# A scan level of 4 tokens back moved from the projections into the scans, queries read in place by the scans' products, and v blocks in the order 0, 2, 1, 3

## The chip, the cores and the metric

The kernel runs on one core of a Trainium2 chip. The metric is the device time of the whole kernel in microseconds (us). The engines are named as in the profile: PE is TensorE's matmul side and PEld its weight loads, DVE is VectorE, ACT is ScalarE, POOL is GpSimd, SP is SyncE, and a q behind a name (SPq, ACTq) is the queue from which that engine issues transfers. Each engine works through its own list of instructions strictly in order, so an instruction that waits holds up what stands behind it on its engine.

## The reference, cut to what matters

One layer on 128 context tokens and 1024 latent tokens, 1024 channels. A combined projection gives, for each of 8 heads of 128 channels, the queries q, two forget gates f (one for each direction), the values v and a gate z. Each direction runs a gated linear recurrence along the tokens:

```
S_t = diag(f_t) S_{t-1} + k_t v_t^T        k_t = 1 - f_t
o_t = S_t^T q_t
```

The reference works in chunks of 32 tokens, in which the pair of a token t and an earlier token s has the weight "q_t times k_s times the product of all f between them":

```
att = einsum('bhtc,bhsc,bhtsc->bhts', qi, ki, decay)
o   = einsum('bhts,bhsv->bhtv', att, vi) + einsum('bhtc,bhcv->bhtv', qi * exp(b), S)
```

A Fourier branch, output gates, two branch projections, one output projection and a norm follow. All of it is in float32.

## The kernel before

**Tiling.** The 1152 tokens are nine chunks of 128. Channels stand on the partitions, tokens on the free axis. Every dense product is split in three: a weight and an input are each a rounded high part and a low rest, and `mm3` (lines 205 to 211) issues high by high, low by high and high by low, in moving pieces of 288 tokens (256 for v).

**Stages.** First the statistics and the normalised input `h1`, `h2`; then the values, `project_v` (from line 398): v block `pr` holds the weights of two heads. The loop over `pr` in 0, 1, 2, 3 calls it; blocks 2 and 3 cover here only the chunks 5 to 8 (`LATE_V`), and the rest is done later among the scans. The split weights of a block (`w_hi` on ACT, line 184, `w_lo` on POOL, line 186) go to the pool `vb` for even and `va` for odd blocks, each with one buffer, so a block whose pool is still read by products has to wait with its split. Beside the v blocks, POOL, DVE and ACT build sums and differences of the input (`r`, line 427; `ts`, line 432; `t0` to `t3`, lines 434 and 435) that the next stage needs. In that stage 27 times `pair` computes two projections by seven products of 24 matmuls (`PRODUCTS`); the weights of a pair arrive as `raw`, are combined on DVE (line 636) and split (lines 618, 619).

**Steps among the projections.** Between the products of a pair the generator `four` is moved on by one step (the line with `next(four, None)`): first the Fourier branch, then `pieces`, which prepares the scans. A piece is one head and either 640 or 512 tokens, so there are 16. It loads f and q back from memory (lines 571 and 574), forms k = 1 - f (`L585`) and q times f (`L586`, `L587`), and then works by levels: the tokens that lie m back, for m = 1, 2, 4, are handled by pairs of blocks of m tokens. A level copies the halves of `kk` and `qq` that it needs side by side (`halves`, L470 on ACT), multiplies keys and queries by the gate product of the block (`grow`, L464 on DVE), doubles the gate blocks (L466), has 20 or 16 small products of 32 by 32 on PE (`within`, L484; each is two instructions in the trace, so x40 or x32), and merges their result by a mask (`merge`, L475 for the diagonal and L477). After the last grow it keeps a thinned gate product `fa` (L599, one in `GRAN` = 8 tokens) and issues the loads of the next piece's f, and after its last products that of the next q.

**The scans.** `scan_blocks` takes a head on from there over the levels 8 and 16 (`LATE`), with copies `km` and `qm` of 1152 tokens on ACT, `grow` over 1152 tokens, and 36 small products (x72), and then the levels 32 and 64, whose products read `kk` and `qq` in place. The state recurrence (`scan_rest`), the last chunks of v and the branch projections (`F`, a group of 12 matmuls of 288 tokens) are mixed with it by the strings of `PATTERN`: each letter moves one generator on by one step (E: blocks, L: the head before, Y: the rest of the head two before, V: late v, F: dense). PE keeps this written order in the scans. On the other engines the order of instructions comes from the scheduler of the framework, by priority and readiness.

Of the kernel before, what the change touches and what calls it, by code (L numbers as in the profile page):

```python
# [48 lines left out]
PRODUCTS = (1, 5, 6, 2, 7, 4, 3)  # L49
EARLY = (1, 2, 4)  # L50
GATES = 6
LATE = (8, 16)
GRAN = 8
PIECES = ((0, 640), (640, T))
PATTERN = (['VEVVEVVEVVEVV', 'VEVLVVLEVVLVVLEVVLVVLELFLF'] + 6 * ['EYLFYLEYLFLEFFFLEFLFLF'] +
           ['YLFYLFYLFLFFFLFLFLF', 'YFYFYFFF'])
# [13 lines left out]
def diffusion_step(ctx: ExitStack, tc: tile.TileContext, xT, x_tok, w_pr, w_v, w_ada, w_ada_gt,  # L70
# [326 lines left out]

    def project_v(pr, chunks):
        raw = vb.tile([P, KT, 2 * P], F32, tag="wr", name="w_raw")
        nc.sync.dma_start(raw, w_v[pr])  # L400
        hi, lo = split_w(raw, KT, 2 * P, (vb, va)[pr % 2])
        for c in chunks:
            ps = dense_ps()[:, :2 * P]
            mm3(ps, [(*h_at(k, c * P, (c + 1) * P), hi[:, k, :], lo[:, k, :]) for k in range(KT)])
            vo = va.tile([P, SW], F32, tag="vo", name="vo", bufs=2)[:, :2 * P].rearrange("p (h v) -> p h v", h=2)
            nc.vector.tensor_copy(vo, ps)
            nc.sync.dma_start(v_dr[2 * pr:2 * pr + 2, :, c, :].rearrange("h p v -> p h v"), vo)
# [8 lines left out]
    with pool("tg", 1, side="right") as tg:  # L416
        for pr in range(NH // 2):
            with tc.issue_after(last_ada[-1].ins):
                project_v(pr, range(5 if pr in LATE_V else 0, NCH))
            for k in ((0,1,2,3), (), (), ())[pr]:  # L420
# [37 lines left out]
    def grow(ff, kk, qq, m, w=T, g=1):  # L458

        n, mg, wg = w // (2 * m), m // g, w // g  # L460
        dims = [[2 * m, n], [w + m, 2], [1, m]]
        for x, off, step in ((qq, wg + mg, -(wg + mg)), (kk, mg, wg - mg)):
            xv = view(x, 0, dims)
            nc.vector.tensor_tensor(out=xv, in0=xv, in1=view(ff, off, [[2 * mg, n], [step, 2], [0, m]]), op=ALU.mult)  # L464
# [149 lines left out]
    with pool("se", 1) as se, pool("sl", 1) as sl_, pool("sp", 1) as sp:  # L614
# [7 lines left out]
        def pair(n, evacs):  # L622
# [40 lines left out]
            for i in PRODUCTS:  # L663
                bank = {5: "d", 3: "d", 2: "b"}.get(i, "a")
                for j in range(2):
# [14 lines left out]
                    elif i == 3:  # L680
                        result(0, 1, j, 6, "d")
                        done(0, j)
                if i in (() if n < 3 else (5, 6, 2, 7, 3) if n < 13 else (5, 2, 7, 3)):
                    next(four, None)
# [84 lines left out]
    def scan_blocks(hd, kk, qq, fa, a32):  # L769

        kk2, qq2 = flat(kk), flat(qq)
        for m in LATE:
            ps = scan_ps()
            km = s0[0].tile([P, T], F32, name="km", bufs=2)
            halves(kk2, km, m)
            qm = s0[0].tile([P, T], F32, name="qm", bufs=1)
            halves(qq2, qm, m)
            grow(fa, kk2, qq2, m, g=GRAN)
            within(ps, km, qm, NCH, matmul)
            merge(a32, m, ps, NCH)  # L780
# [413 lines left out]
```

## Time and profile before

| | us |
|---|---|
| three runs | 1345.76, 1347.02, 1348.8 |
| median | 1347.02 |
| profiled execution, its own time | 1346.88 |
| its span (first to last instruction) | 1345.1 |

The table of the profile's busy times is read per engine against the span, and the same per stretch. The stretches used below are the end of the v blocks (155.7 to 175.5 us), the pairs with the level steps between their products (398 to 830) and the scans (895 to 1150). A row of the waits gives who waited, for what, how long in total, how often, and the longest case. In a timeline row the bracket at the end is the idle time of that engine just before the instruction and what ended it. PEclk is the granted clock of TensorE as a share of full speed.

### The profile page before, as it was taken

To read this page: it belongs to the slowest core of one execution; us is meant where nothing else is said; L and a number is where in the kernel's file an instruction comes from. 1 tells how busy PE (TensorE), PEld (TensorE's weight loads), DVE (VectorE), ACT (ScalarE), POOL (GpSimd) and SP (SyncE) were. 2 spreads that over 40 slices of the span, in tenths; PEclk is the share of its full clock that TensorE was granted. 3 is DMA by queue.
4 is the path that set the end of the run, shared out by engine and by line. 5 is a ranking of instruction groups with operands and counts; after the bars stand their busy time and mean duration, and the time that the engine had idled before them with its cause. 6 is when DMAs were issued, how large, how long until landed. Compare 5 with 4: busy or idle time off the path is not lost.

```text
span 1345.1 us, 31341 instructions
## 1 busy us (share of the span) xinstructions
PE 1257.2 (93%) x12768; PEld 1176.5 (87%) x12768; DVE 842.7 (63%) x1423; ACT 650.8 (48%) x1330; POOL 459.0 (34%) x359
## 2 busy tenths in 40 slices
PE   5999899999999999999999999999999999999998
PEld 3679899999999888888988988898888989989886
DVE  7637843434357767777677766448677777465554
ACT  5442223455446655656556554446655555332332
POOL 4425513224412112122121115512322254564564
PEclk8799899999999999999999999999999999999999
DMA  8541233324444455344543554583767764677332
GB/s 330 195 165 58 85 98 122 133 100 152 150 138 135 161 194 178 133 143 172 185 169 139 178 187 157 211 290 121 258 218 246 242 203 138 197 217 218 130 128 94
DMA packets 126162, 227.52 MB, mean 169 GB/s; under 512 B 15537, under 2 KB 78786, under 8 KB 121794
## 3 DMA queue, kind: packets, MB, share of 16 engines
q1 hardware_dynamic: 125730, 224.47, 49.6%
q8 instruction: 100, 1.64, 0.5%
q10 hardware_dynamic: 288, 1.05, 0.3%
q14 instruction: 44, 0.36, 0.1%
HBM read 153.64 MB, written 71.84 MB: 168 GB/s over the span
## 4 chain that ended last, share of the span: by engine, by line
PE 52%; DVE 18%; DMA 16%; ACT 5%; issue 5%; SPq 2%; POOL 1%; DVEq 0%; ACTq 0%; POOLq 0%
PE d_ps L200 6%; DMA raw<-in_w_pr 6%; PE o_ps L209 6%; PE o_ps L210 6%; PE d_ps L209 6%; PE o_ps L211 5%; PE d_ps L210 5%; PE d_ps L211 5%; PE o_ps L200 5%; DMA qq<-qq_dr 2%; DVE s L636 2%; DVE px L464 2%; DMA pz<-q_dr 2%; DVE pz L464 2%; DVE ts L432 1%
## 5 line engine op out<-in xcount | busy, mean ns | idle before, releaser
L619 POOL TENSOR_TENSOR wl<-raw,wh 128x512 fp32r<-128x512 f32 x81 | 115.8, 1430 | 465.4 <-ACT wh L618 418.4
L619 DVE TENSOR_TENSOR wl<-s,wh 128x512 fp32r<-128x512 f32 x81 | 62.7, 777 | 80.4 <-ACT wh L618 80.2
L186 POOL TENSOR_TENSOR w_lo<-w_raw,w_hi 128x512 fp32r<-128x512 f32 (+1 forms) x36 | 65.0, 1807 | 129.9 <-ACT w_hi L184 129.9
L209 PE MATMUL o_ps<-h1h,wh 128*128 128x288 f32 x324 | 97.1, 300 | 3.7 <-DVE c L656 2.0
L211 PE MATMUL o_ps<-h1h,wl 128*128 128x288 f32 x324 | 96.4, 298 | 2.5 <-POOL wl L619 2.5
L618 ACT CAST wh<-raw 128x512 fp32r<-128x512 f32 x108 | 66.4, 616 | 64.6 <-DMA raw<-in_w_pr 42.9
L210 PE MATMUL o_ps<-h1l,wh 128*128 128x288 f32 x324 | 96.8, 299 | 0.0
L618 ACT CAST wh<-s 128x512 fp32r<-128x512 f32 x81 | 50.2, 620 | 88.3 <-DVE s L636 43.7
L200 PE MATMUL d_ps<-yh,w_hi 128*128 128x288 f32 x256 | 81.5, 318 | 8.5 <-ACT yh L911 2.8
L200 PE MATMUL d_ps<-yl,w_hi 128*128 128x288 f32 x256 | 76.7, 300 | 0.0
L200 PE MATMUL d_ps<-yh,w_lo 128*128 128x288 f32 x256 | 76.7, 299 | 0.0
L928 POOL TENSOR_TENSOR merged<-merged,gs 128x288 f32<-128x288 f32 x64 | 56.0, 887 | 52.4 <-DVE gs L927 52.4
L656 DVE TENSOR_TENSOR c<-o_ps,x 128x288 f32<-128x288 f32 x108 | 47.4, 450 | 34.5 <-PE o_ps L211 28.8
L209 PEld LDWEIGHTS o_ps<-h1h,wh 128*128 128x128 f32 x324 | 61.1, 189 | 5.1 <-ACT wh L618 2.4
L211 PEld LDWEIGHTS o_ps<-h1h,wl 128*128 128x128 f32 x324 | 60.9, 188 | 3.8 <-POOL wl L619 3.5
L464 DVE TENSOR_TENSOR qq<-qq,fa 128x1152 f32<-128x1152 f32 x32 | 47.3, 1478 | 23.9 <-PE s_ps L200 15.7
L210 PEld LDWEIGHTS o_ps<-h1l,wh 128*128 128x128 f32 x324 | 61.0, 188 | 0.5 <-issue 0.3
L200 PEld LDWEIGHTS d_ps<-yh,w_hi 128*128 128x128 f32 x256 | 49.2, 192 | 10.3 <-ACT yh L911 4.7
L636 DVE TENSOR_TENSOR s<-raw 128x512 f32<-128x512 f32 x27 | 27.6, 1021 | 46.9 <-DMA raw<-in_w_pr 46.7
L464 DVE TENSOR_TENSOR pz<-pz,px 128x640 f32<-128x640 f32 (+1 forms) x48 | 53.0, 1103 | 1.9 <-ACT pz L470 1.9
L586 DVE TENSOR_TENSOR px<-pz,px 128x640 f32<-128x640 f32 (+1 forms) x32 | 27.7, 906 | 40.7 <-DMA pz<-q_dr 30.4
L696 POOL TENSOR_TENSOR c<-c,sg 128x576 f32<-128x576 f32 x24 | 39.1, 1629 | 37.9 <-ACT sg L694 35.7
(387 smaller groups left out, 4696.2 us busy)
## 6 DMA issues: line engine op xcount, KB each, us to landing
raw<-in_w_pr SPq DMA_DIRECT2D x52, 512.0 KB, 5.8
gs<-g_dr SPq DMA_DIRECT2D x96, 144.0 KB, 3.2
w_raw<-in_w_pab SPq DMA_DIRECT2D x44, 256.0 KB, 3.6
f_dr<-c SPq DMA_DIRECT2D x32, 288.0 KB, 3.6
kk<-kk_dr SPq DMA_DIRECT2D x8, 1152.0 KB, 7.2
qq<-qq_dr SPq DMA_DIRECT2D x8, 1152.0 KB, 7.2
wa<-in_w_ada SPq DMA_DIRECT2D x8, 1024.0 KB
g_dr<-c SPq DMA_DIRECT2D x28, 288.0 KB, 2.5
```

Of the source, the lines that this page charges most:

```text
L186: eng.tensor_tensor(out=lo, in0=raw, in1=hi.bitcast(F32), op=ALU.subtract)
L200: queued(nc.tensor.matmul(*args, **kw))
L209: mm(out, lhsT=sh, rhs=mh, start=first and i == 0, stop=False, **kw)
L210: mm(out, lhsT=sh, rhs=ml, start=False, stop=False, **kw)
L211: mm(out, lhsT=sl_, rhs=mh, start=False, stop=last and i == n - 1, **kw)
L464: nc.vector.tensor_tensor(out=xv, in0=xv, in1=view(ff, off, [[2 * mg, n], [step, 2], [0, m]]), op=ALU.mult)
L618: nc.scalar.copy(hi, src)
L619: eng.tensor_tensor(out=lo, in0=src, in1=hi.bitcast(F32), op=ALU.subtract)
L636: nc.vector.tensor_tensor(out=out, in0=x, in1=y, op=op)
L656: nc.vector.tensor_tensor(out=c[:, h], in0=ps[bank, j], in1=x[i, j], op=ALU.add)
L696: nc.gpsimd.tensor_tensor(out=c, in0=c, in1=sg, op=ALU.mult)
L928: nc.gpsimd.tensor_tensor(out=out, in0=out, in1=gs, op=ALU.add)
```

## The change

Level 4 leaves the pieces (`EARLY` = 1, 2) and becomes the first level of the scans (`LATE` = 4, 8, 16); the gate product is kept for one in 4 tokens instead of one in 8, so `fa` doubles. In `scan_blocks` the copy `qm` is dropped: the 36 products of 32 by 32 for keys and queries (nine chunks by four) read `qq` through a strided view, and they are written before `grow`, which changes `qq` in place and so has to wait for them. `grow` multiplies the keys first, then the queries. A piece has three steps instead of four, and the steps stand after other products of a pair. The strings of `PATTERN` have one E more in every head, and in the second string fewer V. `project_v` takes the blocks in the order 0, 2, 1, 3, with the pools `vb` and `va` in turn. The amount of products on PE is the same: what leaves a stage is added in another.

```diff
-EARLY = (1, 2, 4)
+EARLY = (1, 2)
-LATE = (8, 16)
-GRAN = 8
+LATE = (4, 8, 16)
+GRAN = 4
-PATTERN = (['VEVVEVVEVVEVV', 'VEVLVVLEVVLVVLEVVLVVLELFLF'] + 6 * ['EYLFYLEYLFLEFFFLEFLFLF'] +
+PATTERN = (['VEVVEVVEVVEVVE', 'VEVLVLEVVLVELVVLEVLFELFLF'] + 6 * ['EYLFYLEYLFELFFFEFLELFLF'] +
            ['YLFYLFYLFLFFFLFLFLF', 'YFYFYFFF'])
...
-    def project_v(pr, chunks):
+    def project_v(pr, chunks, p):
...
-        hi, lo = split_w(raw, KT, 2 * P, (vb, va)[pr % 2])
+        hi, lo = split_w(raw, KT, 2 * P, p)
...
-        for pr in range(NH // 2):
+        for nth, pr in enumerate((0, 2, 1, 3)):
             with tc.issue_after(last_ada[-1].ins):
-                project_v(pr, range(5 if pr in LATE_V else 0, NCH))
+                project_v(pr, range(5 if pr in LATE_V else 0, NCH), (vb, va)[nth % 2])
...
-        for x, off, step in ((qq, wg + mg, -(wg + mg)), (kk, mg, wg - mg)):
+        for x, off, step in ((kk, mg, wg - mg), (qq, wg + mg, -(wg + mg))):
...
-                if i in (() if n < 3 else (5, 6, 2, 7, 3) if n < 13 else (5, 2, 7, 3)):
+                if i in (() if n < 3 else (1, 5, 6, 2, 7, 3) if n < 4 else (5, 6, 2, 7, 3) if n < 7 else (6, 7, 3)):
                     next(four, None)
...
             halves(kk2, km, m)
-            qm = s0[0].tile([P, T], F32, name="qm", bufs=1)
-            halves(qq2, qm, m)
+            for c in range(NCH):
+                for j in range(4):
+                    t0 = c * P + 32 * j
+                    matmul(ps[32 * j:32 * j + 32, c * 32:c * 32 + 32], lhsT=km[:, t0:t0 + 32],
+                           rhs=view(qq2, t0, [[2 * m, 16 // m], [T + m, 2], [1, m]]), start=True, stop=True)
             grow(fa, kk2, qq2, m, g=GRAN)
-            within(ps, km, qm, NCH, matmul)
             merge(a32, m, ps, NCH)
```

Three places show how it moves instructions. The first is DVE in the projections, around the end of a piece of 512 tokens. `pz` holds the keys and `px` the queries and gates of the piece, L619 and L636 are weights of the next products, L656 takes products out of PSUM. Before:

```order
L466 TENSOR_TENSOR px<-px 128x256
L477 COPY_PREDICATED ps<-m_i,s_ps 128x128
L656 TENSOR_TENSOR c<-d_ps,x_7007 128x288
L464 TENSOR_TENSOR pz<-pz,px 128x64x2x4
L464 TENSOR_TENSOR px<-px 128x64x2x4
L466 TENSOR_TENSOR px<-px 128x128
L619 TENSOR_TENSOR wl<-raw,wh 128x512
L477 COPY_PREDICATED ps<-m_i,s_ps 128x128
L619 TENSOR_TENSOR wl<-s_7225,wh 128x512
L586 TENSOR_TENSOR px<-pz,px 128x640 x2
L587 TENSOR_TENSOR pz<-pz 128x640
```

and now:

```order
L466 TENSOR_TENSOR px<-px 128x256
L636 TENSOR_TENSOR s_7174<-raw,s_7174 128x512
L477 COPY_PREDICATED ps<-m_i,s_ps 128x128
L656 TENSOR_TENSOR c<-o_ps,x_6938 128x288
L656 TENSOR_TENSOR c<-d_ps,x_6952 128x288
L586 TENSOR_TENSOR px<-pz,px 128x640 x2
L619 TENSOR_TENSOR wl<-raw,wh 128x512
L587 TENSOR_TENSOR pz<-pz 128x640
L619 TENSOR_TENSOR wl<-s_7174,wh 128x512
```

The two products with blocks of 4, one doubling and one merge are gone, and the first instructions of the next piece (L586, L587) stand ahead of, or between, the low parts of the weights.

The second is DVE in a scan head, from the level of 16 to the level of 32 tokens (the shape ends in the block length). L925 and L845 before are L927 and L847 now: the branch projections' and the state's work. Before:

```order
L464 TENSOR_TENSOR kk<-kk,fa 128x36x2x16
L845 SCALAR_TENSOR_TENSOR S<-S,tot,o_ps 128x128 x4
L464 TENSOR_TENSOR qq<-qq,fa 128x18x2x32
L464 TENSOR_TENSOR kk<-kk,fa 128x18x2x32
L845 SCALAR_TENSOR_TENSOR S<-S,tot,o_ps 128x128 x2
L925 TENSOR_TENSOR merged<-gs,d_ps 128x288
L466 TENSOR_TENSOR fa<-fa 128x36
L925 TENSOR_TENSOR merged<-gs,d_ps 128x288
```

and now:

```order
L464 TENSOR_TENSOR kk<-kk,fa 128x36x2x16
L847 SCALAR_TENSOR_TENSOR S<-S,tot,o_ps 128x128
L464 TENSOR_TENSOR qq<-qq,fa 128x36x2x16
L477 COPY_PREDICATED fa<-m_i,s_ps 128x288
L847 SCALAR_TENSOR_TENSOR S<-S,tot,o_ps 128x128 x2
L927 TENSOR_TENSOR merged<-gs,d_ps 128x288
L466 TENSOR_TENSOR fa<-fa 128x72
L847 SCALAR_TENSOR_TENSOR S<-S,tot,o_ps 128x128 x2
L927 TENSOR_TENSOR merged<-gs,d_ps 128x288
```

The queries of level 16 are multiplied after its keys and beside its merge now, so they stand directly before work that PE waits for (`merged`, which frees a product's bank).

The third is POOL at the end of the v blocks. Before, the low parts of the last block's weights come after the last sums `r`:

```order
L427 TENSOR_TENSOR r<-h2h_150,h2l_151 128x288
L427 TENSOR_TENSOR r<-h1h_142,h1l_143 128x288
L427 TENSOR_TENSOR r<-h2h_158,h2l_159 128x288
L186 TENSOR_TENSOR w_lo<-w_raw,w_hi 128x2048
L619 TENSOR_TENSOR wl<-raw,wh 128x512 x6
```

and now twelve sums earlier:

```order
L427 TENSOR_TENSOR r<-h1h_140,h1l_141 128x288
L427 TENSOR_TENSOR r<-h2h_156,h2l_157 128x288
L186 TENSOR_TENSOR w_lo<-w_raw,w_hi 128x2048
L427 TENSOR_TENSOR r<-h1h_132,h1l_133 128x288
L427 TENSOR_TENSOR r<-h2h_148,h2l_149 128x288
```

The last block's split no longer waits for the end of the long block 1.

## Rows read from the trace of the kernel before

**Rows 1.** The page's first part: busy us, share of the span and instructions

```profile
PE 1257.2 (93%) x12768; PEld 1176.5 (87%) x12768; DVE 842.7 (63%) x1423; ACT 650.8 (48%) x1330; POOL 459.0 (34%) x359
```

**Rows 2.** Busy time of each engine by stretch, then granted clock and DMA

```profile
155.70:175.50 19.80, 12.66 (x93) 12.45 (x93) 15.05 (x21) 4.57 (x9) 7.54 (x4) 0.83 0.30 80
...
398.00:830.00 432.00, 404.83 (x4959) 384.76 (x4957) 316.15 (x488) 253.14 (x460) 92.73 (x60) 0.99 0.46 157
...
895.00:1150.00 255.00, 236.43 (x3609) 227.56 (x3609) 187.29 (x355) 143.69 (x356) 81.79 (x65) 0.97 0.65 209
```

**Rows 3.** PE's waits, 398 to 895: for what, us in total, times, longest

```profile
PE o_ps L209 <- ACT x L646: 4.8, 7, 1.6
PE s_ps L484 <- issue: 4.0, 5, 1.2
PE s_ps L484 <- DVE pz L587: 3.7, 4, 1.8
PE s_ps L484 <- ACT pz L470: 3.4, 4, 1.3
PE s_ps L484 <- DMA pz<-q_dr: 3.3, 2, 1.9
PE o_ps L209 <- DVE c L656: 2.9, 2, 2.0
```

**Rows 4.** Timeline at a piece's start: start us, us, engine, line, operation

```profile
528.44 0.51 ACT L599 COPY ps<-px 128x160 f32<-128x160 f32 x1 [2.85 <-DVE px L466]
...
533.35 1.33 ACT L585 ACTIVATE pz<-px,ones 128x512 f32<-128x512 f32 x2 [3.58 <-DMA px<-f_dr]
...
535.51 0.46 PE L484 MATMUL s_ps<-pz 128*32 128x32 f32 x32 [1.81 <-DVE pz L587]
```

**Rows 5.** Busy time by stretch just before and after that wait

```profile
530.00:533.70 3.70, 3.69 (x28) 3.46 (x26) 0.19 (x1) 0.35 (x1) 0.00 (x0) 1.00 0.91 251
...
537.10:540.50 3.40, 2.94 (x13) 2.60 (x12) 1.56 (x3) 2.41 (x4) 1.28 (x1) 0.50 0.17 64
```

**Rows 6.** Timeline of PE: products of one level, 640 tokens and 1152 tokens

```profile
413.88 0.56 PE L484 MATMUL s_ps<-pz 128*32 128x32 f32 x40
...
1027.70 0.83 PE L200 MATMUL s_ps<-qm,km 128*32 128x32 f32 x72
```

**Rows 7.** Timeline of ACT: copies of levels 1 and 4, 640 tokens

```profile
456.23 1.03 ACT L470 COPY pz<-pz 128x640 f32<-128x640 f32 x1
...
464.59 0.71 ACT L470 COPY pz<-pz 128x640 f32<-128x640 f32 x1
```

**Rows 8.** Busy time by stretch: one scan head

```profile
1022.80:1054.40 31.60, 29.22 (x456) 28.12 (x455) 23.34 (x48) 17.59 (x46) 7.24 (x5) 1.00 0.71 231
```

**Rows 9.** Timeline of PE and DVE in that head

```profile
1040.94 0.37 PE L200 MATMUL d_ps<-yh,w_hi 128*128 128x288 f32 x1 [1.51 <-DVE fa L466]
...
1045.59 1.36 DVE L464 TENSOR_TENSOR qq<-qq,fa 128x1152 f32<-128x1152 f32 x1 [2.31 <-PE s_ps L200]
```

**Rows 10.** Timeline around the last v block

```profile
161.96 0.58 PE L209 MATMUL d_ps<-w_hi,h2h 128*128 128x256 f32 x1 [6.28 <-DVE vo L406]
...
175.54 0.37 PE L209 MATMUL d_ps<-h1h,wh 128*128 128x288 f32 x1 [0.92 <-DVE vo L406]
...
155.81 4.71 POOL L186 TENSOR_TENSOR w_lo<-w_raw,w_hi 128x2048 fp32r<-128x2048 f32 x1
...
156.27 4.57 DVE L432 TENSOR_TENSOR ts<-r,ts 128x288 f32<-128x288 f32 x1
...
160.76 0.45 DVE L432 TENSOR_TENSOR ts<-r 128x288 f32<-128x288 f32 x1
...
162.37 0.87 ACTq L626 DMA_DIRECT2D raw<-in_w_pr  x2
...
168.75 1.15 DVE L636 TENSOR_TENSOR s<-raw 128x512 f32<-128x512 f32 x1 [4.48 <-DMA raw<-in_w_pr]
...
171.14 0.42 DVE L406 COPY vo<-d_ps 128x256 f32<-128x256 f32 x1
```

## The prediction

> **What bounds the kernel now.** I read the page first: PE is busy for 1257.2 us of the span of 1345.1, and no other engine is busy for more than two thirds of it [rows 1]. So the time is PE's work plus PE's waits, about 88 us, and every other engine counts only where PE waits for it. The table by stretch says where those waits are [rows 2]: 19.8 - 12.66 = 7.1 us at the end of the v blocks, 432 - 404.83 = 27.2 us among the projections with level steps, 255 - 236.43 = 18.6 us in the scans. The granted clock is 0.83, 0.99 and 0.97 in these three. The change touches just these three stretches, so I went to the waits of each.
>
> Among the projections PE waits longest for the small products of the levels: four rows of L484 add up to 14.4 us, and the next largest are the evacuations on ACT and DVE with 4.8 and 2.9 [rows 3]. About 11 of the 14.4 us lie at starts of pieces. One of them in the timeline shows the chain [rows 4]: ACT keeps the thinned gate at 528.44 after waiting for DVE's last doubling, SP issues the load of the next f right behind that, ACT gets it at 533.35, DVE's k stands after that, and PE starts at 535.51 after 1.81 us of nothing. The chain is 7 us long, most of it the load, so it is not the work of an engine but the distance between a piece's last grow and the next piece's first product that decides. Two of the longest such waits are followed by 3.4 us at a granted clock of 0.50, the lower of the two levels (1.2 instead of 2.4 GHz) [rows 5]; each costs 1.7 us more.
>
> In the scans a head takes 31.6 us, with PE busy for 29.22 and DVE for 23.34 [rows 8]. PE's longest wait in it is 1.51 us for DVE [rows 9]; DVE in turn sits idle for 2.31 us before the queries' product of level 64, until PE has read them in place [rows 9]; the other heads have about the same there.
>
> **Products that move.** A level of a piece is 0.56 us on PE for 640 tokens [rows 6] and 0.46 us for 512 [rows 4]; of a whole head in the scans it is 0.83 us [rows 6]. Eight heads leave 8 x (0.56 + 0.46) = 8.2 us in the projections and add 8 x 0.83 = 6.6 us to the scans: **-1.6 us**. PE has no cover in either stretch, so both count in full.
>
> **Reading the queries in place.** No row shows small products with a moving operand in runs of 4, 8 or 16 tokens. From below they cost nothing more: the operand has the same 32 columns, and nothing is left out, so no gain is possible on PE. From above I take ACT, which reads through the same kind of view: 1.03 us in runs of one token against 0.71 us in runs of four [rows 7], a ratio of 1.45. At 1.45 the 24 blocks would cost 24 x 0.83 x 0.45 = 9.0 us more. I take 0, as the copies show the loss at runs of one and have lost most of it at four, which is the shortest run here; the 9 us stay as a rival. A sentence beside this: the Trainium skill, page "SBUF — State Buffer", section "Door 1: The DMA port swizzle", says that SBUF has lines of 16 bytes and that four float32 in a row can be strided without loss; by that the term would be 0 as well, by the ACT ratio +9, and no row of TensorE here settles it.
>
> **Starts of pieces.** Level 4 goes from each of the 16 pieces: per head two copies of 0.7 us and less on ACT [rows 7], four products, two doublings and two merges on DVE. Counted in PE's order, the last grow of a piece and the first product of the next stood 145 instructions apart on average (the level's own 40 among them), and stand 151 apart now (36 of the level). That is ten dense instructions more, at 3.70 / 28 = 0.13 us each [rows 5] about 1.3 us of extra time for a chain that stays 7 us long. 15 waits of 0.2 to 1.9 us (0.7 on average) against 1.3 us: at best some 9 of 11 us go. But the load's landing varies by more than a microsecond, and L586 and L587 now stand ahead of weights on DVE, so that a late load holds those up too. I take half, **-5 us** (-1 to -9). The other waits at level products, 14.4 - 11 = 3.4 us, occur at 48 blocks instead of 64: **-1**. The evacuation waits of 4.8 + 2.9 us [rows 3] arise behind copies and grows on the in-order queues of ACT and DVE, of which a third disappears: **-2.5** (0 to -5). With one of the two clock drops gone: **-1.7** (0 to -3.4). What is late next is the weights' chain (load, DVE, ACT, low part), which already shows as small waits of PE.
>
> **v blocks.** PE has nothing for 6.28 us until 161.96 and then does the last block at half clock; the first pair starts at 175.54 [rows 10]. The new order splits the last block's weights long before (POOL has them twelve sums earlier), so the block follows the long one without a gap and PE is through by about 167. But the first pair has its own chain: its weights are requested by ACT at 162.37, behind ACT's last `t`, and DVE starts on them at 168.75 [rows 10]. The pair also needs the banks of the v blocks, and on DVE one copy `vo` of them stands behind three combinations of these weights, before (at 171.14, [rows 10]) as after: 171.14 + 0.42 - 168.75 = 2.8 us more, so the pair can't start before about 171.6. The split of 4.71 us on POOL, beside which a 0.45 us subtraction of DVE takes 4.57 [rows 10], now falls in the middle of the chain of sums instead of at its end; I let it delay the chain by 0 to 2 us. The first pair then starts at 171.6 to 173.6 instead of 175.54: **-3 us** (0 to -6). Most of PE's gap only changes places. Had the split no effect on DVE, the chain would be 4 us shorter and the gain at the upper end, near 6. The row has it (4.57 beside 4.71); a rule that says the same is in the Trainium skill, "SBUF — State Buffer", section "Who interferes with whom": a DVE operation with two inputs from SBUF and a GpSimd operation that reads it exclude each other for a whole instruction.
>
> **Scans.** Each head gets one level more on DVE: two products of 1.36 us [rows 9] and with the doubling and merge, which I estimate at 0.45 each, some 3.6 us; 23.3 becomes 27 of PE's 29.2 + 0.83 = 30.1. It no longer waits for the copies `qm`, but for PE: the queries may only be changed after the products that read them. So what waits on PE is the queue behind that product on DVE, `merged` and the state, and PE waits for those to free its banks. Between level 32 and level 64 PE has 19 dense instructions, 2.5 us, while DVE does two grows of 1.36: 0.2 to 0.6 us of a new stall per head, and the wait of 1.51 us [rows 9] has no reason to shrink. I take 0.5 us per head: **+4** (0 to +12, the upper end being another 1.51 per head).
>
> **Sum.** -1.6 - 5 - 1 - 2.5 - 1.7 - 3 + 4 = -10.8 us. The profiled execution took 1346.88 us, 1.8 more than its span and within 0.2 of the median 1347.02, so the sum can be set against either: 1346.9 - 10.8 = **1336 us**. The ends of the terms taken all together are 1320 and 1357; a more likely spread is 1326 to 1343.
>
> **Rival 1: the piece waits stay (1346 us).** If the load and not the distance sets the start (it is issued later relative to PE, or lands later because it meets other transfers), then -5, -1, -2.5 and -1.7 vanish, and 1336 + 10.2 = 1346 is left. For it: the chain of 7 us is untouched. Against it: the distance grows and ACT and DVE have less to do. Chance 0.16.
>
> **Rival 2, slower: DVE becomes the bound in the scans (1354 us).** DVE's idle time in a head is 31.6 - 23.34 = 8.3 us, 2.31 of it the wait at the level read in place [rows 8, 9]. Now three more levels are read in place. If these waits keep DVE's idle time at 8.3 us, a head becomes 3.6 us longer instead of 0.83 + 0.5, over eight heads 28.8 instead of 10.6: 1336 + 18 = 1354. It decides as soon as DVE can't bring its idle time below 31.6 + 0.83 - 27, or 5.4 us a head. For it: each queries' product stands behind one more product of PE. Against it: `qm` copies and their waits go, the keys' product goes first, and PE's blocks are early in its order. Chance 0.16.
>
> **Rival 3: the strided reading costs (1345 us).** The 9 us of above: 1336 + 9 = 1345. Chance 0.07.
>
> **How the numbers follow.** The forecast has 0.61. About 0.2%, 2.7 us, is what a measurement of this kernel can tell from no change. Rivals 1 and 3 lie within it, rival 2 beyond. Faster: 0.61 and some of rivals 1 and 3, together 0.64; same 0.18; slower 0.18. The range has to hold rivals 1 and 3 and the forecast's own spread, and leaves out rival 2 and the far lower end: 1325 to 1350.
>
> **What would show it.** Right: the four L484 rows fall from 14.4 to about 8 us, no half clock follows a piece's start, the first pair starts before 174 with PE's gap after the last v block instead of ahead of it, and a middle head of the scans takes 31 to 32 us with DVE busy for about 27. Wrong: L484 waits as before with SP's load at the end of their chain (rival 1); heads of 35 us with PE waiting for `merged` or `qq` (rival 2); 72 small products in 1.2 us instead of 0.83 (rival 3). The forecast fails above all if PE's new stalls in the scans exceed 1.5 us a head.

## The result, and the profile after

The changed kernel took 1336.05 us (median of 20 runs, 1332.06 to 1345.96), the kernel before 1346.72 (20 runs). The ratio is 0.9931, with a 95% interval of 0.9915 to 0.9946, so 7 to 11 us less. The forecast was 1336, the range 1325 to 1350. The total came out as predicted, in part by luck: most terms were off in size, the clock had the wrong sign, and the errors cancelled.

The first profiled execution of the changed kernel happened to be its longest run (1345.96 us), so the rows here come from a second profile of the same kernel (1339.91 us, label e0_again below). The two traces differ most in the clock: among the pairs TensorE ran for 20.5 us at a granted clock of 0.50 in the first and for 13.7 us in the second.

The page's first part, as in [rows 1]:

```profile
PE 1251.2 (94%) x12768; PEld 1174.7 (88%) x12768; DVE 836.9 (63%) x1391; ACT 627.9 (47%) x1290; POOL 474.6 (35%) x359
```

PE's busy time has hardly changed (1257.2 before); nothing in the change removes products. The gain shows only by stage. From the third pair of projections to the last, and from there to the last level of the scans, the kernel before has these two rows (start and end, length, busy us of PE, PEld, DVE, ACT and POOL, granted clock, DMA share, GB/s):

```profile
221.60:893.90 672.30, 640.95 (x6672) 614.64 (x6671) 411.23 (x644) 363.88 (x685) 175.26 (x126) 0.99 0.47 161
893.90:1138.70 244.80, 226.23 (x3526) 217.43 (x3525) 179.86 (x342) 136.82 (x333) 74.49 (x58) 0.97 0.67 214
```

and the changed kernel these:

```profile
220.50:872.50 652.00, 629.76 (x6096) 610.30 (x6095) 369.67 (x580) 348.33 (x653) 177.89 (x126) 0.99 0.50 168
872.50:1133.30 260.80, 233.91 (x4125) 221.94 (x4125) 216.74 (x376) 131.38 (x328) 89.30 (x60) 0.99 0.63 207
```

The pairs became 672.3 - 652.0 = 20.3 us shorter, 11.2 of it busy time and 9.1 idle time of PE. The scans became 16.0 us longer, 7.7 busy and 8.3 idle; 1.6 us of that is a group of dense products that the strings moved here from behind the last level. The spans of the two traces differ by 7.0 us in all; the 2.7 us that these stretches leave lie in the start and the tail, where single runs differ by some us (the first product of v comes between 82.9 and 87.7 us in the traces of this study).

PE's waits in the pairs, which answer to [rows 3]:

```profile
PE s_ps L484 <- issue: 6.2, 4, 2.1
PE o_ps L209 <- DVE c L656: 3.7, 4, 1.3
PE o_ps L209 <- DVE pz L587: 2.5, 1, 2.5
PE s_ps L484 <- DVE pz L587: 2.3, 1, 2.3
PE s_ps L484 <- ACT pz L470: 2.2, 3, 1.0
PE d_ps L209 <- ACT x L646: 2.0, 2, 1.6
```

and three of the kernel before that [rows 3] leaves out:

```profile
PE o_ps L211 <- POOL wl L619: 2.5, 4, 0.8
PE d_ps L209 <- DVE c L656: 2.3, 6, 0.7
PE d_ps L209 <- ACT x L646: 1.8, 2, 1.3
```

The L484 rows are 6.2 + 2.3 + 2.2 = 10.7 us against 14.4. A wait put down to "issue" has no releaser in the profile; the one of 2.13 us at 563.50 ends right behind DVE's `pz` of L587, which stood behind a late f. The evacuations on ACT and DVE (L646, L656), 4.8 + 2.9 + 2.3 + 1.8 = 11.8 us before, are 7.0 with two rows of 1.0 and 0.3. The waits for low weights `wl` are gone. And there is a row that was not there before: products that wait for `pz` of L587.

The v blocks, which answer to [rows 10] (start, length, engine, line, operation; in the bracket the idle time ahead and its end):

```profile
138.29 4.60 POOL L186 TENSOR_TENSOR w_lo<-w_raw,w_hi 128x2048 fp32r<-128x2048 f32 x1 [0.30 <-ACT w_hi L184]
...
138.58 4.63 DVE L435 TENSOR_TENSOR t3l<-ts,t3h 128x288 fp32r<-128x288 f32 x1 [1.47 <-ACT t3h L434]
...
162.96 0.88 ACTq L626 DMA_DIRECT2D raw<-in_w_pr  x2
...
169.30 1.15 DVE L636 TENSOR_TENSOR s<-raw 128x512 f32<-128x512 f32 x1 [4.44 <-DMA raw<-in_w_pr]
...
172.26 0.58 PE L209 MATMUL d_ps<-h1h,wh 128*128 128x288 f32 x1 [5.61 <-DVE vo L406]
```

The split on POOL has moved to 138.29, a DVE subtraction beside it takes 4.63 us instead of the 4.57 of before at the end, ACT asks for the first pair's weights at 162.96, and the first pair starts at 172.26 instead of 175.54. PE's gap, 5.61 us, now lies behind the last v block. What the gap does next is in the stretches of the first pair:

```profile
172.30:177.70 5.40, 5.40 (x23) 5.40 (x24) 3.98 (x7) 0.97 (x3) 1.42 (x1) 0.50 0.22 65
177.70:197.20 19.50, 19.50 (x148) 19.50 (x148) 6.12 (x11) 6.12 (x13) 3.00 (x3) 1.00 0.29 99
```

After the gap PE runs at a granted clock of 0.50 for 5.4 us, and these are now products of the first pair, which takes 24.9 us; before it took 198.0 - 175.5 = 22.5, since the half clock fell on the gap itself and on the last v block.

A middle head of the scans, from its first block product to the next head's, and its wait before the level of 64 tokens, which answer to [rows 8, 9]:

```profile
977.90:1009.50 31.60, 29.93 (x532) 28.85 (x532) 28.76 (x53) 17.27 (x46) 10.36 (x6) 1.00 0.71 235
...
1000.87 0.83 PE L200 MATMUL s_ps<-qq,kk 128*64 128x64 f32 x21 [1.67 <-DVE qq L464]
```

Three middle heads in a row take 31.6, 30.6 and 32.4 us; before they took 30.3, 31.6 and 29.9, so the head of [rows 8] was the longest of its three. DVE is busy for 28.76 us in the head shown, 23.34 in that of [rows 8]. PE waits 1.67 us for `qq` before the level of 64 tokens; the wait of 1.51 us for `merged` and `fa` ahead of the third group of dense products is gone. Over the three heads PE's idle time is 4.2 us as before: there the waits only changed places.

The new idle time lies in the second head, whose string was rewritten as well. It is shown before and now, with PE's longest waits in it now:

```profile
921.60:954.60 33.00, 33.00 (x498) 32.26 (x497) 23.05 (x43) 19.54 (x45) 8.82 (x8) 1.00 0.49 151
```

```profile
897.20:942.30 45.10, 38.13 (x586) 36.23 (x588) 32.53 (x51) 20.16 (x44) 13.17 (x8) 0.96 0.45 147
```

```profile
PE o_ps L200 <- DVE S L847: 2.4, 1, 2.4
PE d_ps L200 <- ACT w_hi L184: 1.9, 1, 1.9
PE d_ps L200 <- DVE vl L750: 1.1, 1, 1.1
```

PE had no idle time there and has 7.0 us now, of the 8.3 us that the scans gained. It is 6.9 to 8.0 us in all nine traces with the added level and 0.2 at most in the four without. Whether the level or its string makes it was not tried.

### The profile page after: what moved, and what is told of

It reads as the page before. It is cut to its first block, busy times and chain, and to the rows that moved or that the text cites. A ratio compares the mean times of both kernels' runs of the same rounds, so it can differ in the third digit from the quotient of the medians.

```text
span 1344.2 us, 31219 instructions
## 1 busy us (share of the span) xinstructions
PE 1260.1 (94%) x12768; PEld 1183.8 (88%) x12768; DVE 836.3 (62%) x1391; ACT 628.7 (47%) x1290; POOL 479.4 (36%) x359
## 4 chain that ended last, share of the span: by engine, by line
PE 50%; DMA 12%; DVE 10%; issue 5%; ACT 3%; POOL 2%; SPq 1%; DVEq 0%; POOLq 0%; ACTq 0%
PE o_ps L210 7%; PE o_ps L209 7%; PE o_ps L211 7%; PE d_ps L209 5%; PE d_ps L211 5%; PE d_ps L210 5%; DMA raw<-in_w_pr 4%; PE d_ps L200 4%; PE o_ps L200 3%; DMA ya_dr<-gz 2%; DMA wr<-in_w_o 2%; DMA px<-f_dr 1%; PE s_ps L547 1%; DMA yr<-ya_dr 1%; PE s_ps L200 1%
## 5 line engine op out<-in xcount | busy, mean ns | idle before, releaser
L619 POOL TENSOR_TENSOR wl<-raw,wh 128x512 fp32r<-128x512 f32 x81 | 119.5, 1476 | 444.5 <-ACT wh L618 422.3
L619 DVE TENSOR_TENSOR wl<-s,wh 128x512 fp32r<-128x512 f32 x81 | 60.8, 755 | 80.9 <-ACT wh L618 80.7
L930 POOL TENSOR_TENSOR merged<-merged,gs 128x288 f32<-128x288 f32 x64 | 64.4, 1018 | 62.5 <-DVE gs L929 59.2
L656 DVE TENSOR_TENSOR c<-o_ps,x 128x288 f32<-128x288 f32 x108 | 47.8, 450 | 53.1 <-PE o_ps L211 43.2
L464 DVE TENSOR_TENSOR kk<-kk,fa 128x1152 f32<-128x1152 f32 x40 | 58.9, 1476 | 14.9 <-PE s_ps L200 8.6
L464 DVE TENSOR_TENSOR qq<-qq,fa 128x1152 f32<-128x1152 f32 x40 | 63.7, 1593 | 0.5
L636 DVE TENSOR_TENSOR s<-raw 128x512 f32<-128x512 f32 x27 | 27.6, 1020 | 55.6 <-DMA raw<-in_w_pr 55.6
L586 DVE TENSOR_TENSOR px<-pz,px 128x640 f32<-128x640 f32 (+1 forms) x32 | 23.8, 785 | 53.0 <-DMA px<-f_dr 31.7
L184 ACT CAST w_hi<-w_raw 128x512 fp32r<-128x512 f32 (+1 forms) x48 | 34.8, 725 | 40.6 <-DMA w_raw<-in_w_pab 10.5
```

Of the source, the lines that this page charges most:

```text
L184: nc.scalar.copy(hi, raw)
L619: eng.tensor_tensor(out=lo, in0=src, in1=hi.bitcast(F32), op=ALU.subtract)
L636: nc.vector.tensor_tensor(out=out, in0=x, in1=y, op=op)
L656: nc.vector.tensor_tensor(out=c[:, h], in0=ps[bank, j], in1=x[i, j], op=ALU.add)
L930: nc.gpsimd.tensor_tensor(out=out, in0=out, in1=gs, op=ALU.add)
```

## The experiments

The kernel before, timed beside each group of runs, took 1344.7 to 1345.2 us (medians); ratios are to it.

**The changed kernel again (e0_again).** No edit.

> The changed kernel once more, as the yardstick of this group and for a second trace. Its profiled execution above was the longest of its runs (1345.96 us against a median of 1336), so the theory that late loads make the difference expects a profiled time near 1336 to 1340, the same first pair at 171 to 172 us, and fewer waits of TensorE behind DMA in the pairs (L484 and the products behind pz and c, 19 us in the first trace) and in the scans (w_hi, w_lo, gs: 13 us). The rival, that these waits belong to the kernel's order, expects the same waits at the same instructions and a time near 1346 again in the profile.

Measured: 1336.17 us, ratio 0.9911 (0.9881 to 0.9941). The profiled execution took 1339.91 us, the upper end of what the theory named. The products behind `pz` of L587 waited again at the same pair (3.7 us in the first trace, 2.5 here, 2.0 to 2.7 in four later traces of these pairs), the waits at piece starts again took 2 us and more, while the waits for `w_hi` and `w_lo` in the scans fell from 9.3 to 3.8 us. So the first two recur with this order, and the last differ from run to run.

**The v order alone (e1_v_order).** The kernel before with

```diff
-        for pr in range(NH // 2):
+        for nth, pr in enumerate((0, 2, 1, 3)):
...
+                project_v(pr, range(5 if pr in LATE_V else 0, NCH), (vb, va)[nth % 2])
```

> The kernel before with the v blocks in the order 0, 2, 1, 3 and their pools in turn, nothing else. Theory: this part is separate and worth what the first pair gains, 175.5 to about 171.4 us, so about -4 us (ratio 0.9970). Rival: the level move is a wash and the whole gain of 9 us comes from here, for instance because the clock or the loads of the pairs fall better; then about 0.993. Second rival: the gain at the first pair is lost again in the next pairs, since PE's gap only moves; then 1.000.

Measured: 1344.74 us, ratio 0.9992 (0.9970 to 1.0014). The theory's -4 us lies at the very edge of the interval and the second rival within it, so the time alone leaves anything from no gain to 4 us. The trace shows more; its first pair starts at 172.97 after 6.22 us of nothing, and takes 24.90 us:

```profile
173.00:197.90 24.90, 24.90 (x168) 24.90 (x169) 10.12 (x18) 7.09 (x16) 4.36 (x4) 0.89 0.28 92
```

Counted from each trace's first product of v, the first pair starts after 83.8 to 85.8 us in the nine traces with the new order (mean 85.0) and after 87.3 to 88.5 us in the four with the old one (mean 88.1), so 3.1 us earlier; the second pair after 109.7 and 110.5 us on average, 0.8 us earlier. These means mix kernels with four and with five buffers of split weights; this run against the kernel before alone has 2.6 us at the first pair and less than 0.1 at the second. Most of what the order gains, the half clock takes back within one pair.

**The level move alone (e2_levels).** The changed kernel with these lines of `project_v` and its loop as before.

> The changed kernel with the v blocks in the old order and with the old pools, so the level move alone. Theory: -5 us (ratio 0.996): projections shorter by 8.2 us of products and 3 to 5 us of waits, scans longer by 6.6 us of products and about 1 us. Rival (wash): 1.000, projections shorter by 12 us and scans longer by as much. Rival (all of it): 0.993.

Measured: 1334.68 us, ratio 0.9908 (0.9880 to 0.9937). The whole gain is here, more than the theory's 5 us. The trace has 649.6 us for the third to the last pair (652.0 with both parts, 672.3 before).

**The scans without the added level (e3_no_scan_level).** The level of 4 tokens is left out of the result.

```diff
-LATE = (4, 8, 16)
+LATE = (8, 16)
```

with the strings of `PATTERN` as before.

> The changed kernel without the level of 4 tokens in the scans (that level is left out of the result), and with the old strings for the scans. Against the changed kernel it gives what the added level costs there. Theory: products 6.6 us and 0.5 us of new waits a head, together 8 to 11 us, so about 1326 us (ratio to before 0.985). Rival, VectorE's load is the price in the scans (3.6 us a head): 25 to 29 us, so about 1309 us (0.972). Rival, no new waits at all: 6.6 us, 1329.5 us.

Measured: 1324.86 us, ratio 0.9838 (0.9812 to 0.9863). The level and its strings together cost 1336.2 - 1324.9 = 11.3 us in the scans (by the two intervals some 5 us more or less), at the upper edge of the theory's 8 to 11 us and far from the 25 to 29 us of the rival. Its scans, to be held against the second row of the changed kernel above:

```profile
871.20:1118.30 247.10, 223.92 (x3527) 215.18 (x3525) 186.50 (x342) 120.64 (x317) 80.72 (x58) 0.97 0.66 217
```

Of 13.7 us less, 10.0 are busy time (1.6 of it the group that the strings move) and 3.7 idle time, although 17.1 us of these scans ran at half clock and only 6.8 us of the changed kernel's.

**Contiguous reading (e4_contiguous).** The levels' products read other queries than they should, so their result is another.

```diff
-                           rhs=view(qq2, t0, [[2 * m, 16 // m], [T + m, 2], [1, m]]), start=True, stop=True)
+                           rhs=qq2[:, t0:t0 + 32], start=True, stop=True)
```

> The changed kernel, but the 36 products of a level in the scans read 32 queries that stand side by side instead of the halves of the blocks through the strided view (so those levels' result is another one; count, size and waits are the same). It prices the strided reading alone. Theory: it costs nothing, so the same time as the changed kernel within 1 us and 0.83 us for a group of 72. Rival (by the ratio of ACT's copies): 9 us faster, with the groups at 0.57 us here or at more than 0.83 in the changed kernel.

Measured: 1336.42 us (0.9891 to 0.9956 of before) against 1336.17. The products by line and shape (busy us, mean ns), first of the changed kernel, then of this one:

```profile
L200 PE MATMUL s_ps<-qq,km 128*32 128x32 f32 x1728 | 20.3, 199 | 4.2 <-issue 1.8 <-DVE qq L464 1.5 <-ACT km L470 0.9
```

```profile
L200 PE MATMUL s_ps<-qq,km 128*32 128x32 f32 x1728 | 20.3, 199 | 3.8 <-issue 2.1 <-ACT km L470 0.9 <-DVE qq L464 0.8
```

Both 20.3 us for 1728 instructions: the strided reading in runs of 4, 8 and 16 tokens costs nothing here, and rival 3 of the prediction is out.

**The load of f a piece earlier (e6_four_bufs and e5_early_f).** For space, both have four buffers of split weights instead of five; the second also has

```diff
+        fb = [x[:, 0], sp.tile([P, 1024], F32, name="fx")]
...
             nc.vector.tensor_tensor(out=k0, in0=kk[:, :w], in1=kk[:, w:], op=ALU.add)
+            if i + 1 < len(todo):
+                load_f(*todo[i + 1])
             yield
...
-                        if i + 1 < len(todo):
-                            load_f(*todo[i + 1])
```

where `load_f` and the piece use the two buffers `fb` in turn.

> The changed kernel with four instead of five buffers for the split weights of a pair, nothing else: the yardstick for the run with the early load, which needs their space. Expected: the same time within 3 us, since a pair uses seven products' weights one after the other and PE waited for weights only 2 us in the pairs.

> As the run with four buffers, but the f of the next piece goes to a second buffer and is requested a whole piece earlier, so the chain grow, thinned gate, load, k is gone from the starts of pieces; the load of q stays. Theory of the prediction (this chain makes the waits at piece starts, and DVE's instructions behind it wait too): L484 waits fall from about 11 us to 3 us or less, the wait of products behind pz is gone, and the time falls by 6 to 10 us against the run with four buffers. Rival: the waits are those of the q load, or of in-order work on DVE and ACT ahead of k; then the time stays within 2 us and L484 waits as before. Second rival: the clock gives nothing back, so 11 us of waits make 8 us.

Measured: 1335.56 us with four buffers (0.9930, 0.9902 to 0.9957), 1319.00 with the early load (0.9802, 0.9774 to 0.9830). So the early load alone takes off 16.6 us, about twice the theory's amount, and the rivals are out. In the two traces 13.8 us of the difference lie in the pairs. The pairs of the yardstick, then those with the early load, and PE's waits there:

```profile
215.90:867.70 651.80, 631.06 (x6096) 610.51 (x6095) 376.75 (x581) 349.92 (x654) 177.63 (x126) 0.99 0.49 168
```

```profile
217.20:855.20 638.00, 625.78 (x6096) 606.20 (x6095) 372.56 (x581) 351.28 (x654) 175.54 (x126) 1.00 0.50 172
```

```profile
PE o_ps L209 <- DVE c L657: 3.7, 5, 1.4
PE o_ps L209 <- ACT wh L619: 3.3, 2, 1.8
PE d_ps L209 <- ACT x L647: 1.8, 2, 1.4
PE d_ps L209 <- DVE c L657: 1.2, 1, 1.2
PE s_ps L484 <- DMA pz<-q_dr: 0.9, 2, 0.5
```

No L484 wait but 0.9 us is left (6.0 with four buffers). The wait of dense products behind `pz` is in neither of the two traces; in the yardstick a load of f holds up an evacuation instead: at 477.89 ACT begins k after 4.18 us of waiting for f, its copy `x` stands behind that, and PE waits 3.36 us for the copy. Idle time falls from 20.7 to 12.2 us. Busy time falls too, from 631.06 to 625.78, although the products are the same: the time at half clock in this stretch is 13.7 us in the one trace and 3.4 in the other, half of which is lost. So against the second rival the clock gives 5 us on top of the 8.5 us of waits. Two later traces with the early load have no half clock in the pairs at all, seven traces of the changed pairs without it 0 to 20.5 us.

**One F moved in the scans (e7_pattern).**

```diff
-6 * ['EYLFYLEYLFELFFFEFLELFLF']
+6 * ['EYLFYLEYLFELFFEFFLELFLF']
```

> The changed kernel with one of the three F groups between levels 16 and 32 moved to between levels 32 and 64 in the six middle heads. In the changed kernel PE waits for the queries' product of level 32 (s_ps behind qq, 4.4 to 5.7 us in all, 1.4 to 1.7 a head), as 19 dense products are too few to cover two grows on DVE. Theory: 12 more products (1.6 us) cover it and the time falls by 4 to 8 us, to about 1330. Rival: DVE is what bounds the head, so the wait only moves to another place (merged, S or the level of 32) and the time stays within 2 us.

Measured: 1336.25 us, ratio 0.9940 (0.9917 to 0.9963): no gain. PE's longest waits in its scans, and under them the same two rows of the changed kernel:

```profile
PE o_ps L200 <- DVE S L847: 8.7, 5, 2.4
PE s_ps L200 <- DVE qq L464: 3.9, 4, 1.5
```

```profile
PE s_ps L200 <- DVE qq L464: 7.0, 8, 1.7
...
PE o_ps L200 <- DVE S L847: 2.4, 1, 2.4
```

The wait for `qq` went from 7.0 to 3.9 us, and the one for the state `S` from 2.4 to 8.7. The time is the rival's, and the rows fit it: what is taken from one wait comes back in the other. That DVE has as much to do as PE between the products that make the state and the first that read it is my reading, which no run shows by itself.

**The early load in the kernel before (e8_before_early_f).** The same buffers in the kernel before, with the request behind the first grow of a piece, as the f of the next head is not yet there earlier.

> The kernel before with four weight buffers and the f of the next piece loaded into a second buffer, requested after the first grow of a piece instead of after the last. It asks what the level move is worth once no piece waits for its f. Theory: the move's gain in the pairs is 11 us of products and turn-around and some 10 us of waits and half clock; the scans give back 14 us. With the waits gone anyway, the move costs 3 us, so this kernel comes out at 1315 to 1320 us, level with the changed kernel with the early load (1319) or better. Rival: the level's other work on ACT and DVE makes the waits, so the early load helps less here (-5 to -8 us against before, about 1338) and the move keeps its 9 us and more.

Measured: 1334.26 us, ratio 0.9933 (0.9908 to 0.9958). My theory falls; the time is nearer to the rival's 1338. The early load is worth 11 us here and 17 in the changed kernel; the level move and the v order together are worth 15 us (0.9933 to 0.9802) with the early load and 9 without. The pairs take 664.9 us in this trace against 638.0, and PE's first waits there are others:

```profile
PE o_ps L209 <- ACT wh L619: 5.0, 3, 2.0
PE s_ps L484 <- ACT pz L470: 4.6, 7, 1.5
PE s_ps L484 <- DMA pz<-q_dr: 4.3, 7, 1.1
```

Although the request stands later here than in the changed kernel, ACT waits for f nowhere in this trace (55.8 us in the kernel before). With four levels in a piece ACT's copies (L470) and the load of q become the last to arrive once f does not. So f was not the only wait at the level products; 8.9 us are left with four levels a piece and 0.9 with three. Which of the two holds the other up was not tried. Yet in the traces these waits are not what makes 11 us of the one and 17 of the other. The pairs here:

```profile
220.80:885.70 664.90, 641.90 (x6671) 618.01 (x6671) 408.70 (x645) 365.07 (x686) 182.60 (x126) 0.99 0.48 163
```

The early load takes 8.4 us of PE's idle time out of the pairs of the kernel before (31.4 to 23.0) and 8.5 out of those of the changed kernel. What differs is the clock: the time at half clock goes from 6.8 to 17.1 us here and from 13.7 to 3.4 there. These are single traces.

**The early load with the old v order (e9_early_f_old_v).** The changed kernel with the early load, the loop of the v blocks as before.

> The changed kernel with the early load of f (1319.0 us), but the v blocks in the old order. From the traces the order brings the first pair 3.1 us forward and the second only 0.7, since the half clock after PE's gap then falls on the first pair's products. Theory: 0 to 1 us slower, so the same within the measurement. Rival: the order is worth the 3 us of the prediction, so 1322.

Measured: 1321.38 us, ratio 0.9829 (0.9800 to 0.9858). The difference to 1319.0 is 2.4 us, and the two intervals overlap. It does not decide between 1 us and 3. With the old v order on both sides the early load is worth 1334.7 - 1321.4 = 13.3 us in the changed kernel, and the level move alone 1334.3 - 1321.4 = 12.9 us with it and 10.2 without; that is not clear of the 11 and 10 us that plain adding would give.

**The early load and a fifth group (e10_early_f_pattern).**

```diff
-6 * ['EYLFYLEYLFELFFFEFLELFLF']
+6 * ['EYLFYLEYLFELFFFEFFLELLF']
```

> The changed kernel with the early load of f, and in the six middle heads one F from the end of the head moved to between levels 32 and 64, so that five groups of dense products instead of four stand between the state's products and the first that read the state. When one was moved from between 16 and 32, the wait went from qq (7.0 to 3.9 us) to S (2.4 to 8.7 us). Theory: DVE has too much to do between those two places, and 1.6 us more of products there cover both waits: -4 to -7 us, about 1313. Rival: the F is missing at the end of the head, where PE then waits for ACT's copies and DVE's scaling: 1319 to 1322.

Measured: 1321.80 us, ratio 0.9828 (0.9802 to 0.9855): the rival's time, though not its place. PE's longest waits in its scans are now for the weights of the dense groups:

```profile
PE d_ps L200 <- POOL w_lo L186: 7.1, 3, 3.5
PE d_ps L200 <- ACT w_hi L184: 6.6, 3, 2.8
```

The waits for `S` and `qq` are 4.4 us together there, 9.2 with the early load alone, and these weights' rows 13.7 us instead of 3.8. That the moved group makes them late is not shown: the same rows came to 9.3 and 3.8 us in two traces of the changed kernel. The kernel with the early load alone, 1319.0 us, has the lowest median of the study; it is ahead of both kernels compared.

## Why the prediction was right, point by point

**Products that move: -1.6, the sign right, the size too small.** Per level I took the block's busy time alone (0.56 and 0.46 us). The rows around one block in the changed kernel show what it costs beside that:

```profile
402.33 0.29 PE L211 MATMUL o_ps<-h1h,wl 128*128 128x288 f32 x1
402.55 0.56 PE L484 MATMUL s_ps<-pz 128*32 128x32 f32 x40
403.04 0.40 PE L209 MATMUL d_ps<-t3h,wh 128*128 128x288 f32 x1
403.27 0.29 PE L210 MATMUL d_ps<-t3l,wh 128*128 128x288 f32 x1
403.40 0.29 PE L211 MATMUL d_ps<-t3h,wl 128*128 128x288 f32 x1
```

It begins 0.22 us after the product before it instead of 0.13, the next product 0.49 later, and the one after that 0.23 later instead of 0.13: 0.68 us for 640 tokens, and by the same turn-around some 0.58 for 512. 8 x 1.26 = 10.1 us leave the pairs, not 8.2. The traces have more than that. Half of the time at half clock is lost (6.8 us of it in the pairs before and 13.7 now, 17.1 and 6.8 in the scans); without that loss PE's busy time fell by 11.2 + 3.4 = 14.6 us in the pairs and grew by 7.7 + 5.1 = 12.8 in the scans, 1.6 of these for the moved group. The blocks explain 10.1 and about 7 us (0.83 to 0.92 each there). Where the other 4 us of either come from no run shows.

**Reading in place: 0, right**, by e4_contiguous. The sentence of the Trainium skill, "SBUF — State Buffer", section "Door 1: The DMA port swizzle", on four float32 in a row agrees: 0.83 us a group with either reading.

**Starts of pieces: -5 and -1, right in the cause, wrong in the size.** L484 went from 14.4 to 10.7 us, while I expected 8. The cause I named, the chain to the load of f, is shown by e5_early_f: with the load out of the way, these waits vanish. But at the starts of pieces they only became fewer and longer: eleven of 0.2 to 1.9 us (10.9 together) before, five of 0.8 to 2.3 us now and one of 2.5 us behind `pz`, 11 us again. The -1 for the other level products came (3.4 to 2.2 us). The step that failed is that the chain stays 7 us long: from the thinned gate to ACT's k it takes 7.2 us on average over 15 pieces instead of 6.7, and 10.1 at most instead of 8.4, so the ten dense instructions that I added to the distance did not cover it. The prediction also named what would spoil it: L586 and L587 now stand ahead of weights and evacuations on DVE, so that a late load holds them up. That is the new row, seen here in the timeline:

```profile
485.40 1.56 DVE L586 TENSOR_TENSOR px<-pz,px 128x640 f32<-128x640 f32 x2 [4.32 <-DMA px<-f_dr]
...
486.95 0.83 DVE L587 TENSOR_TENSOR pz<-pz 128x640 f32<-128x640 f32 x1
...
487.77 0.40 PE L209 MATMUL o_ps<-t3h,wh 128*128 128x288 f32 x1 [2.55 <-DVE pz L587]
```

DVE waits 4.32 us for f, and PE's products for what stands behind it, 2.55 us.

**Evacuations: -2.5, mis-sized.** They went from 11.8 to 7.0 us, which is -4.8. I had counted two of the four rows. The waits for `wl`, 2.5 + 0.5 = 3.0 us before and none now, stood in no term.

**Clock: -1.7, the wrong sign.** I expected one of two half-clock stretches in the pairs to go. There are four of 3.4 us now, each close behind a wait of 1.7 to 2.6 us (two of them here, after the waits of 2.55 and 2.13 us), while two other waits of 2.0 and 2.3 us are followed by none:

```profile
488.40:491.80 3.40, 3.40 (x41) 3.34 (x28) 2.27 (x5) 1.71 (x3) 0.00 (x0) 0.51 0.17 57
563.40:566.90 3.50, 3.40 (x44) 3.37 (x45) 3.15 (x6) 1.81 (x6) 1.28 (x1) 0.51 0.00 1
```

So the clock cost 3.4 us more instead of 1.7 less. Single traces differ widely: seven of these pairs have 0 to 20.5 us at half clock, 12.2 on average, and two of the pairs before 6.8 and 3.4. The one with none, e3_no_scan_level, has waits of up to 2.7 us among them.

**v blocks: -3, right to the first pair, wrong to the end.** The first pair came forward by 3.3 us, as worked out. The step that failed is that I stopped there: I wrote that PE's gap only changes places and did not price the half clock that moves with it. By the second pair 0.8 us is left, and the run with this part alone shows no gain that can be measured. The part on the split holds: with its 4.60 us on POOL beside a DVE subtraction of 4.63 in the middle of the chain, ACT asks for the first pair's weights 75.9 to 76.5 us after the first product of v, instead of 75.2 with the old order, so 0.7 to 1.3 us later where I allowed 0 to 2. The rule of the Trainium skill, "SBUF — State Buffer", section "Who interferes with whom", agrees with these two durations as with those of before (4.71 and 4.57).

**Scans: +4, the sum near, the place right only in part.** With its strings the level costs 11.3 us (e3_no_scan_level) where 6.6 + 4 = 10.6 were forecast. There are new waits between the levels 32 and 64, but they are 0 to 1.7 us a head, 4.2 us over the eight, not 0.2 to 0.6 in each, and the old wait of 1.51 us went in the middle heads, though I saw no reason for that. What PE's idle time gained in the scans, 8.3 us, lies for 7.0 us in the second head, behind the state and the weights of dense products, where I had no term. So the sum is near by luck.

**Sum.** The pairs gave 20.3 us where 8.2 + 5 + 1 + 2.5 + 1.7 = 18.4 stood in the prediction: 14.6 from products instead of 8.2, 9.1 from waits instead of 8.5 (but from evacuations and `wl`, not from piece starts), and 3.4 lost to the clock instead of 1.7 gained. The scans took 11.3 us by the run times, 16.0 - 1.6 = 14.4 by the two traces, where 10.6 were foreseen. The v order gave 0.8 us by the second pair instead of 3. That the total came out within 1 us owes much to these errors cancelling. The ends 1320 and 1357 do not follow from the ranges of the terms, which give 1321 and 1355; nothing else rests on them.

**The rivals.** Rival 1 (piece waits stay) was true of the waits themselves: 10.7 of 14.4 us stayed and 2.5 came back behind `pz`. The pairs still got shorter in other ways, so its 1346 us did not come. Rival 2 did not come, but was near: DVE is busy for 28.8 of 31.6 us in a middle head, and in e7_pattern a wait that was shortened came back elsewhere. Rival 3 is out.

## What to carry to other kernels

A wait that a load causes was best taken away here by requesting the load earlier into a second buffer; that was worth 17 us in the changed kernel and 11 in the kernel before, while thinning the work around it left the same 11 us of waits at piece starts. Where a group of small products is moved, price it from the product before it to the second one behind it: that came to 0.68 us here where the group's own row shows 0.56. Price a change at the head of a stage to the end of the next one: the half clock that followed PE's gap moved with the gap. And look at every head of a repeated stage, not at one in the middle: most of the new idle time of the scans was in the second.

## What had not been expected

The time at half clock does not go with the sum of the waits: the stretch of the pairs with 31 us of idle time had 6.8 us at half clock before, and the changed kernel with 22 us of idle time had 13.7. There it began close behind single waits of 1.7 to 2.6 us, but not behind every one of them, and one trace of the same pairs has waits like these and no half clock. What decides between them stays open. With the early load the pairs had 12 us of idle time and 3.4 at half clock, so over a third of that run's gain in the pairs is clock.

The effects of two parts may not add: the level move and the v order are worth 9 us alone and 15 with the early load, and the early load 11 us in the kernel before and 17 in the changed one. In the traces the early load removes as much idle time of PE in both (8.4 and 8.5 us), and the clock makes the difference. Which operations were late next (ACT's copies and the load of q, in 7 cases each) was visible in the waits only once the first was gone.
